# Out-projection of a hybrid backbone step: products take six PSUM banks in turn instead of three

## The chip, the cores and the metric

The kernel runs on one core of a Trainium2 chip. The core has five engines that work from queues of their own: TensorE (PE, matrix products), VectorE (DVE), ScalarE (ACT), GpSimd (POOL) and SyncE (SP, which only issues DMAs here). They share an on-chip memory (SBUF), and PE writes its results to PSUM, eight banks of which each holds 128 x 512 numbers of 32 bits. The metric is the device time of one execution in microseconds (us).

## The reference

One step of a backbone with three parallel token mixers for 128 prompt tokens and 2048 sample tokens, with a width of 1024. The change touches its end alone: the merged branches go through one output projection, the result is scaled by a gate and added to the input, and a last normalisation follows.

```python
    merged = jnp.einsum('btnd,btnd->btd', gt, pb)
    return jnp.einsum('btd,de->bte', merged, w_out), s_f, s_b
...
        h = h + gate[:, None, :] * out
    y_sample = rmsnorm(h, final_g)
```

## The kernel before

All large products are made of 16-bit operands. Each operand is split into a high and a low part, and a product is the sum of three matmuls (high x high, high x low, low x high) for each block of 128 of the inner dimension. The stages follow each other: weights and norms, the input projection with the three mixers (the delta rule's scan runs beside them, paced by hand), the merge, which projects the three branches, weighs them by their gates and writes the merged rows to DRAM (`mrg`), and last the out-projection.

**The out-projection.** The 2048 sample rows are 16 tiles of 128, taken in eight pairs (`PAIRS`: tiles 8 to 15, then 0 to 7). A pair is one loop turn and is computed as a 2 x 2 block product by Strassen's scheme in Winograd's form, in seven products where eight would be needed. `formed(slot, w)` makes one of them: it takes a PSUM bank and issues twelve matmuls of 128 x 128 by 128 x 512 into it. The left operands lie in one half of `xl` (`v`, slots 0 to 6), the right operands in `gq` (weights kept in SBUF) or in `tw` (three weight sums that come back from DRAM into the place of `xh`). The products are asked for in the order of slots 0, 4, 1, 3, 5, 6, 2; slots 3, 5 and 2 use `tw`.

What empties a bank: `joined` (L1738, on DVE) adds a product times `minv` to rows or to a temporary; `held` (L1733, on ACT) copies the first product of a pair out. `added` (POOL) adds temporaries of SBUF to rows. `final` squares the finished rows (ACT, L1696), takes the root (L170, L171), scales them (DVE, L1701) and stores them.

**Work ahead.** While pair i is multiplied, the generator `coming()` is advanced by one step in each product: `pair_operands` forms the 16-bit operands of pair i + 1 in the other half of `xl` (`halved`: L1601 on ACT, L1602 on DVE), and `pair_sums` takes the next pair but one, whose merged rows `m_load` fetches: squares for the scale (L1590, ACT), a reduction (L1591, DVE), and sums of blocks (L1611 to L1614, POOL). The scale itself comes from `scales`: DVE casts the sums of squares to 16 bits (L175, tile `mscb`), PE adds them over the partitions with one matmul of 128 x 1 against ones, and DVE derives the scale (L185 to L189, L1595). That small matmul is the **norm sum** of the pair; `keep=True` holds it at its place in the program.

**What sets the order.** A scheduler orders each engine's queue when the program is built; `tc.high_priority()` around `joined` and `held` and `keep_in_program_order` on some instructions bind it. At run time each engine takes its queue in order, and an instruction waits for semaphores of others.

**The banks.** Six banks hold products: `ps_mm` is one pool of three, and `ps_d` is a list of three pools of one each. Two more (`ps_x`) hold small results such as the norm sums. `bank` takes the next of `ps_d` by the counter `rot`:

```python
        if pl is ps_d:
            rot[0] += 1
            pl = ps_d[rot[0] % 3]
```

Behind the last pair the 128 prompt rows are multiplied with weights scaled block by block (`ublocks`), two times 96 matmuls of 128 x 128 in two banks of `ps_mm`; gate, residual and norm of these rows end the program.

## Time and profile before

| what | us |
|---|---|
| median of three runs | 2180.36 |
| the three runs | 2178.57 to 2188.07 |
| the profiled execution | 2179.54 |
| its span in the profile | 2177.8 |
| PE busy over the span | 2106.6 |
| first product of the out-projection starts | 1997.56 |
| matmuls of 128 x 512 there | 672 |

The span goes from the first to the last instruction of the profiled execution; 1.7 us lie around it. PE counts as busy while any matmul runs, and matmuls overlap, so the busy times of groups of matmuls are not the time that one takes from start to start. Idle time stands in square brackets behind the instruction that ended it, with what released it. All products and norm sums have line L161, the helper that issues matmuls, and are told apart by their tiles.

### The profile page before, as it was taken

How to read it: one execution, taken by the hardware profiler on the slowest of the kernel's cores; microseconds unless marked ns; L12 is line 12 of the kernel's file. 1: busy time of each engine (PE TensorE's matmuls, PEld its weight loads, DVE VectorE, ACT ScalarE, POOL GpSimd, SP SyncE). 2: the span in 40 equal slices, each digit the busy share in tenths (PEclk: the TensorE clock that was granted, in tenths of full speed). 3: DMA queues.
4: the chain of work that ended last, by engine and by line, in shares of the span. 5: the costliest groups of instructions: out<-in, count | busy, mean ns of one | idle time of the engine just before them, and what ended most of it. 6: DMA issues, size and time to landing. Idle time of an engine off the chain costs nothing.

```text
span 2177.8 us, 43136 instructions
## 1 busy us (share of the span) xinstructions
PE 2106.6 (97%) x16275; PEld 1213.6 (56%) x16275; DVE 1412.6 (65%) x3239; ACT 1059.3 (49%) x2462; POOL 730.9 (34%) x873
## 2 busy tenths in 40 slices
PE   7999999999999998999899999999999999999998
PEld 3555444455555587778556556555654444444344
DVE  5746855469978698676665546756664546654775
ACT  3644644345565574554544445755543335323542
POOL 1431533233333324323322223344542222224652
PEclk9999999999999999999999999999999999999999
DMA  8424733266877664444655555867665557534554
GB/s 279 141 92 142 270 112 113 67 200 210 272 219 252 191 193 149 122 127 142 191 183 161 156 165 181 251 186 223 187 193 174 172 157 212 181 126 162 183 172 152
DMA packets 321499, 384.54 MB, mean 177 GB/s; under 512 B 40721, under 2 KB 227322, under 8 KB 318858
## 3 DMA queue, kind: packets, MB, share of 16 engines
q1 hardware_dynamic: 306090, 321.59, 47.9%
q0 software_dynamic: 12752, 51.27, 6.5%
q10 hardware_dynamic: 2448, 8.91, 1.0%
q8 instruction: 128, 2.10, 0.4%
q14 instruction: 81, 0.66, 0.1%
HBM read 246.72 MB, written 134.96 MB: 175 GB/s over the span
## 4 chain that ended last, share of the span: by engine, by line
PE 45%; DVE 7%; DMA 5%; issue 2%; ACT 2%; POOL 1%; SPq 0%; POOLq 0%; DVEq 0%; ACTq 0%
PE b L161 45%; DVE xl L1602 1%; DMA st<-br 1%; DMA mt<-mrg 1%; DVE XB L799 0%; DVE E L800 0%; DMA wst<-in_w_branch_dram 0%; DMA mrg<-mrow 0%; DMA wst<-in_w_in_dram 0%; DMA ES<-ei 0%; DMA skn<-kv 0%; ACT big L1361 0%; DVE S L912 0%; DMA S<-in_state_delta_dram 0%; DMA sq__2210_18514<-qT 0%
## 5 line engine op out<-in xcount | busy, mean ns | idle before, releaser
L161 PE MATMUL b<-xh,whi 128*128 128x512 f16 (+1 forms) x1920 | 651.4, 348 | 1.0 <-ACT sg L1391 0.7
L161 PE MATMUL b<-xl,whi 128*128 128x512 f16 (+1 forms) x1920 | 651.7, 348 | 0.0
L161 PE MATMUL b<-xh,wlo 128*128 128x512 f16 (+1 forms) x1920 | 650.7, 348 | 0.0
L161 PEld LDWEIGHTS <-whi 128*128 128x128 f16 x3840 | 352.2, 98 | 318.4 <-issue 4.8
L161 PEld LDWEIGHTS <-wlo 128*128 128x128 f16 x1920 | 188.4, 98 | 173.8 <-issue 0.8
L161 PE MATMUL b<-big,bhi 128*128 128x512 f16 (+1 forms) x960 | 249.9, 347 | 1.0 <-ACT big L1361 0.8
L161 PEld LDWEIGHTS <-xl 128*128 128x128 f16 x1488 | 139.8, 98 | 107.3 <-issue 18.3
L1402 POOL TENSOR_TENSOR mrow<-mrow,sg 128x512 f32<-128x512 f32 (+1 forms) x80 | 101.5, 1271 | 275.1 <-DVE sg L1401 212.9
L161 PE MATMUL b<-big,blo 128*128 128x512 f16 (+1 forms) x480 | 163.1, 347 | 0.0
L1391 ACT ACTIVATE sg<-b,winv 128x512 f32<-128x512 f32 (+1 forms) x120 | 74.2, 618 | 140.8 <-PE b L161 140.1
L648 POOL TENSOR_TENSOR cy<-cy,raw 128x545 f32<-128x545 f32 (+1 forms) x48 | 73.3, 1555 | 184.2 <-ACT raw L647 184.2
L161 PEld LDWEIGHTS <-xh 128*128 128x128 f16 x1496 | 118.1, 98 | 28.0
L161 PEld LDWEIGHTS <-bhi 128*128 128x128 f16 x960 | 86.6, 98 | 76.4 <-issue 1.5
L211 ACT ACTIVATE wlo<-wst 128x1024 f16<-128x1024 f32 x52 | 55.0, 1058 | 94.7 <-DMA wst<-in_w_in_dram 92.7
L868 POOL COPY T<-ES 32x256 f16<-32x256 f16 x68 | 28.5, 419 | 216.0 <-DMA ES<-ei 208.4
L1401 DVE SCALAR_TENSOR_TENSOR sg<-b,binv,sg 128x512 f32<-128x512 f32 (+1 forms) x80 | 53.3, 666 | 66.1 <-PE b L161 60.6
L161 PE MATMUL b<-whi,xh 128*128 128x128 f16 x544 | 94.8, 221 | 0.0
L161 PE MATMUL b<-wlo,xh 128*128 128x128 f16 x544 | 94.7, 221 | 0.0
L161 PE MATMUL b<-whi,xl 128*128 128x128 f16 x544 | 94.6, 221 | 0.0
L175 DVE CAST wscb<-wss 128x1 bf16<-128x1 f32 x85 | 12.9, 153 | 122.4 <-ACT wlo L211 76.7
L225 DVE SCALAR_TENSOR_TENSOR wlo<-wst,wsc,whi 128x1024 f16<-128x1024 f32 x52 | 70.1, 1353 | 30.7 <-ACT whi L224 29.6
L161 PE MATMUL b<-gq,xl 128*128 128x512 f16 x384 | 85.7, 379 | 1.8 <-DVE hh L1738 1.0
(500 smaller groups left out, 4318.9 us busy)
## 6 DMA issues: line engine op xcount, KB each, us to landing
wst<-in_w_in_dram SPq DMA_DIRECT2D x60, 512.0 KB
qkv<-cy POOLq DMA_DIRECT2D x12, 1089.0 KB, 5.2
st<-br SPq DMA_DIRECT2D x48, 256.0 KB
mrow<-mrg SPq DMA_DIRECT2D x16, 576.0 KB
dc<-dec SPq DMA_DIRECT2D x17, 512.0 KB
kq<-qkv SPq DMA_DIRECT2D x34, 256.0 KB
kv<-tok POOLq DMA_DIRECT2D x17, 512.0 KB, 5.6
n<-n SPq DMA_DIRECT2D x34, 256.0 KB
```

The source lines that it names most:

```text
L161: return PE.matmul(out, l, r, start=start, stop=stop)
L175: V.tensor_copy(sb16, ss)
L211: A.activation(w.lo, st, AF.Square, accum_out=ss)
L225: V.scalar_tensor_tensor(w.lo, st, s, w.hi, ALU.mult, ALU.subtract)
L648: G.tensor_tensor(y[:, c0:c1], y[:, c0:c1], raw[:, 1 + c0:1 + c1], ALU.mult)
L868: G.tensor_copy(T16[rows(a0, b), :, :, b], ES[0:32, :, 2 * a0 + b, :, wT])
L1391: A.activation(sg, ps, AF.Sigmoid, scale=gw.inv)
L1401: V.scalar_tensor_tensor(sg, ps, binv[:, 1:2], sg, ALU.mult, ALU.mult)
L1402: G.tensor_tensor(mr, mr, sg, ALU.add)
L1602: V.scalar_tensor_tensor(lo, src, s, hi, ALU.mult, ALU.subtract)
```

## The change

`formed` no longer tests the counter `rot`, which `bank` moves too. It has a counter of its own, `turn`, that goes 1, 0, 1, 0 and picks `ps_mm` or `ps_d`. Nothing else is edited; lines behind the first hunk move by one.

```diff
     L, R = slice(0, 512), slice(512, D)
+    turn = [0]
     for i_, (ta, tb) in enumerate(PAIRS):
...
         def formed(slot, w):
-            rot[0] += 1
-            ps = bank(ps_mm if rot[0] % 2 else ps_d, [P, 512])
+            turn[0] ^= 1
+            ps = bank(ps_mm if turn[0] else ps_d, [P, 512])
             for k in range(4):
```

The queues of the built programs show what follows from it. First PE, from the fifth product of pair 1 to the second of pair 2, the first row of each product and the norm sum between. A name such as `b_25999` is one product's bank in one use, `xl` the left operand, `gq` or `xh` the right one (`xh` holds `tw`), and `DVE_49` the semaphore that DVE counts up. Before:

```order
L161 MATMUL b_25999<-xh_93,xl_94 128x512 [waits DVE_49]
...
L161 MATMUL b_26022<-gq_23213,xl_94 128x512 [waits DVE_49]
...
L161 MATMUL b_26053<-xh_93,xl_94 128x512 [waits DVE_49]
...
L161 MATMUL b_26083<-gq_23213,xl_94 128x512 [waits DVE_49]
...
L161 MATMUL b_26035<-mscb_26036,ones_2_89 128x1 [waits DVE_49]
...
L161 MATMUL b_26108<-gq_23213,xl_94 128x512 [waits DVE_49]
```

The same place of PE's queue in the changed program:

```order
L161 MATMUL b_25999<-xh_93,xl_94 128x512
...
L161 MATMUL b_26022<-gq_23213,xl_94 128x512
...
L161 MATMUL b_26053<-xh_93,xl_94 128x512 [waits DVE_49]
...
L161 MATMUL b_26083<-gq_23213,xl_94 128x512 [waits DVE_49]
...
L161 MATMUL b_26035<-mscb_26036,ones_2_89 128x1 [waits DVE_49]
...
L161 MATMUL b_26108<-gq_23213,xl_94 128x512
```

The order is the same; three of five products lose their wait for DVE, and the norm sum, in the middle of a product, keeps its own.

Second PE at the end of the loop: the last pair (`b_26901` to `b_26999`) and the first half of the prompt rows' product (`b_27028`, whose weights `whi`, `wlo` are `ublocks`). Before:

```order
L161 MATMUL b_26901<-gq_23213,xl_94 128x512 [waits DVE_49]
...
L161 MATMUL b_27028<-whi_26881,t_3376_26737 128x128 [waits DMAHW5_49]
...
L161 MATMUL b_26918<-gq_23213,xl_94 128x512 [waits DVE_49]
...
L161 MATMUL b_26947<-xh_93,xl_94 128x512 [waits DVE_49]
...
L161 MATMUL b_27028<-wlo_26882,t_3376_26737 128x128
...
L161 MATMUL b_26999<-xh_93,xl_94 128x512 [waits DVE_49]
...
L161 MATMUL b_27028<-whi_26885,t_3376_26737 128x128 [waits DMAHW7_49]
```

In the changed program:

```order
L161 MATMUL b_26901<-gq_23213,xl_94 128x512
...
L161 MATMUL b_26918<-gq_23213,xl_94 128x512
...
L161 MATMUL b_26947<-xh_93,xl_94 128x512 [waits DVE_49]
...
L161 MATMUL b_26999<-xh_93,xl_94 128x512 [waits DVE_49]
...
L161 MATMUL b_27028<-whi_26881,t_3376_26737 128x128 [waits DVE_49]
...
L161 MATMUL b_27028<-whi_26885,t_3376_26737 128x128 [waits DMAHW7_49]
```

Nine of the prompt rows' matmuls stood between the last products; now all 96 of the first half stand behind them.

Third DVE in pair 1, where the operands of pair 2 are formed (L1602) and the products of pair 1 are joined (L1738 before, L1739 now):

```order
-L1602 SCALAR_TENSOR_TENSOR xl_94<-mt_25776,msc_25879,xl_94 128x4x128
-L1738 SCALAR_TENSOR_TENSOR hh_25919<-b_25965,minv_25677,hh_25919 128x512
-L1602 SCALAR_TENSOR_TENSOR xl_94<-mt_25776,msc_25879,xl_94 128x4x128
+L1739 SCALAR_TENSOR_TENSOR hh_25919<-b_25965,minv_25677,hh_25919 128x512
+L1602 SCALAR_TENSOR_TENSOR xl_94<-mt_25776,msc_25879,xl_94 128x4x128 x2
 L1602 SCALAR_TENSOR_TENSOR xl_94<-ost_25906,msc_25879,xl_94 128x4x256
```

One `joined` stands ahead of one L1602 where it stood behind it. It is the only change of order on DVE. On PE there is one more: in pair 0 two matmuls of the sixth product go ahead of the fifth. ACT, POOL and SP have the same order as before.

## The prediction

> **What bounds the kernel now.** I read the page first, then the stage of the change: windows, waits of TensorE (PE), PE's timeline, and what VectorE (DVE) does where PE waits. The page's first table and its chain that ended last:

> ```profile
> PE 2106.6 (97%) x16275; PEld 1213.6 (56%) x16275; DVE 1412.6 (65%) x3239; ACT 1059.3 (49%) x2462; POOL 730.9 (34%) x873
> PE 45%; DVE 7%; DMA 5%; issue 2%; ACT 2%; POOL 1%; SPq 0%; POOLq 0%; DVEq 0%; ACTq 0%
> ```

> PE is busy 97% of the span, so PE bounds the kernel, and only time that PE loses can be won. The out-projection runs from about 1997 us to the end. The windows (columns: length, busy of PE, PEld, DVE, ACT and POOL, granted clock, DMA share, GB/s) show where PE loses some there:

> ```profile
> 1950.00:2000.00 50.00, 50.00 (x262) 23.80 (x261) 15.48 (x26) 14.87 (x30) 19.84 (x20) 1.00 0.36 115
> 2000.00:2050.00 50.00, 43.37 (x199) 19.07 (x198) 35.70 (x52) 21.79 (x40) 28.95 (x24) 1.00 0.68 231
> 2050.00:2100.00 50.00, 46.06 (x199) 20.06 (x198) 40.35 (x59) 22.45 (x46) 31.87 (x24) 0.93 0.51 163
> 2100.00:2150.00 50.00, 49.55 (x238) 22.66 (x237) 38.04 (x65) 21.45 (x39) 21.88 (x19) 1.00 0.60 211
> ```

> PE stands idle 6.6, 3.9 and 0.5 us in these stretches, and in one its clock is below full. PE's waits between 1780 us and the end, whole:

> ```profile
> PE b L161 <- DVE hh L1738: 7.2, 7, 2.8
> PE b L161 <- DVE sg L1738: 1.9, 2, 1.1
> PE b L161 <- DVE xh L1738: 1.9, 1, 1.9
> ```

> Ten waits, 11.0 us, each for a `joined` (L1738), the DVE instruction that empties a bank: the waits for one of three banks. PE's timeline with the longest of them, with the tiny norm sums (`mscb`) that stand in PE's queue, and with the first and last work of the stage (columns: start, length, work, count, idle time before and releaser):

> ```profile
> 1997.56 7.93 PE L161 MATMUL b<-gq,xl 128*128 128x512 f16 x36
> 2007.41 5.34 PE L161 MATMUL b<-xh,xl 128*128 128x512 f16 x24 [1.92 <-DVE xh L1738]
> ...
> 2022.95 0.17 PE L161 MATMUL b<-mscb,ones 128*128 128x1 bf16 x1
> ...
> 2040.52 0.17 PE L161 MATMUL b<-mscb,ones 128*128 128x1 bf16 x1
> ...
> 2049.26 7.03 PE L161 MATMUL b<-xh,xl 128*128 128x512 f16 x24 [2.07 <-DVE hh L1738]
> ...
> 2060.42 0.17 PE L161 MATMUL b<-mscb,ones 128*128 128x1 bf16 x1
> ...
> 2072.91 7.03 PE L161 MATMUL b<-xh,xl 128*128 128x512 f16 x24 [2.80 <-DVE hh L1738]
> ...
> 2082.36 0.17 PE L161 MATMUL b<-mscb,ones 128*128 128x1 bf16 x1
> ...
> 2112.13 5.34 PE L161 MATMUL b<-xh,xl 128*128 128x512 f16 x24 [0.45 <-DVE hh L1738]
> ...
> 2164.16 5.52 PE L161 MATMUL b<-mt,t 128*128 128x128 f16 x96
> ```

> A 128x512 matmul takes (7.93 - 0.38)/35 = 0.2157 us from start to start, a product of twelve 2.59. After the gaps of 2.07 and 2.80 us 24 matmuls take 7.03 us instead of 5.34, because the clock is halved for 3.4 us; after 1.92 us it is not:

> ```profile
> 2049.80:2053.20 3.40, 3.40 (x10) 1.21 (x8) 3.40 (x5) 3.31 (x9) 1.93 (x1) 0.50 0.97 320
> 2073.65:2077.06 3.41, 3.41 (x10) 1.22 (x9) 3.00 (x3) 0.00 (x0) 2.14 (x3) 0.50 0.54 162
> 2007.40:2012.00 4.60, 4.59 (x22) 2.11 (x22) 2.69 (x4) 0.00 (x0) 1.26 (x1) 1.00 0.51 162
> ```

> So PE loses 11.0 us of waits, 10 x 0.16 (a matmul's modelled end lies 0.16 behind the next one's start) and 2 x 1.69 for the clock: 16.0 us. Check: from 1997.56 to 2164.16 are 166.6 us; 56 products, 7 norm sums of 0.03 and the first 96 small matmuls of the tail (0.056 each, from the last row) are 150.5. **16.0 us is the most that more banks can bring.**

> **The change part by part.** It adds and removes no instruction on any engine. The old counter goes up once in `formed` and once more in `bank`, so it is even at every test and each product takes one of the three `ps_d` banks; the new one really alternates. A bank then comes free after six products, not three.

> The order of work moves in three places, each at no cost. Two matmuls go ahead of a neighbour product: same work. One `joined` goes before an L1602 on DVE (0.7 us each); the operand written there belongs to the next pair. At the end, nine small matmuls no longer stand between the last products: the last product then has 192 small matmuls behind it (10.7 us) where it had 183, so the last rows' norm and store keep their cover. No queue of DMAs changes.

> What is late next? With banks free, PE runs to the norm sums: `scales` keeps its matmul in program order, and PE takes its queue in order, so all products behind a norm sum wait for it. It needs DVE's cast of `mscb`:

> ```profile
> 2022.05 0.16 DVE L175 CAST mscb<-mss 128x1 bf16<-128x1 f32 x1
> ...
> 2039.27 0.16 DVE L175 CAST mscb<-mss 128x1 bf16<-128x1 f32 x1
> ...
> 2058.22 0.14 DVE L175 CAST mscb<-mss 128x1 bf16<-128x1 f32 x1
> ...
> 2072.12 0.73 DVE L1738 SCALAR_TENSOR_TENSOR hh<-b,minv,hh 128x512 f32<-128x512 f32 x1
> ...
> 2076.67 0.14 DVE L175 CAST mscb<-mss 128x1 bf16<-128x1 f32 x1
> ```

> DVE runs late by itself here: in the chain of waits nearly all between 2001 and 2073 is DVE, POOL and DMA, hardly any PE. I take the casts at their present times. From DVE's end to PE's start are 0.06 us (2072.12 + 0.73 to 2072.91), so a cast at 2022.05 of 0.16 lets PE go at 2022.27. PE's way through the four marks, without waits for banks:

> Mark 1: 9 products from 1997.56 end at 2020.86; the cast lets PE go at 2022.27, idle 1.41.

> Mark 2: 66 matmuls on, 2036.54; cast 2039.49, idle 2.95. More than 2.07, so the clock drops: 1.69.

> Mark 3: 70 matmuls and 1.69 on, 2056.31; cast 2058.42, idle 2.11.

> Mark 4: 80 matmuls on, 2075.71, or 2077.40 if 2.11 us idle halves the clock too; cast 2076.87.

> The 2.11 us lie between the two gaps that decide (1.92 and 2.07 as listed are 2.08 and 2.23 between the work itself). Two rows are little to set a limit by, so I take the costlier end, the drop. PE then passes mark 4 at 2077.40 where it was 2082.36: 4.96 us won, 5.49 without the drop.

> [...]

> Behind mark 4 two waits are left, both 0.45 (the second is the row at 2112.13), 0.61 with the 0.16 each: 1.22. They go, if DVE follows. The next cast and a `joined` that waits for PE:

> ```profile
> 2085.25 0.75 DVE L1738 SCALAR_TENSOR_TENSOR hh<-b,minv,hh 128x512 f32<-128x512 f32 x1 [0.51 <-PE b L161]
> ...
> 2097.12 0.14 DVE L175 CAST mscb<-mss 128x1 bf16<-128x1 f32 x1
> ```

> At 2085.25 DVE waits for PE, so from there it moves up with PE. If it didn't, the cast would hold PE at 2097.32 where PE passed at 2101.13: 3.8 us stay, plus 0.61 behind it. That is the low end, 4.4.

> Do six banks suffice? Tightest is product 6 of pair 3: it reuses the bank of that pair's first product, emptied at 2072.85, and starts 68 matmuls behind mark 3, at 2073.1 or 2074.8. It fits. And the first weights from `tw`, which PE now wants at 2005.3?

> ```profile
> 1995.56 1.43 SPq L1679 DMA_DIRECT2D xh<-tw  x3
> ...
> 1996.00:2003.00 7.00, 7.00 (x34) 3.17 (x33) 6.54 (x11) 3.98 (x6) 4.04 (x5) 1.00 0.92 338
> ```

> The rows before them (1 MB) and the first megabyte take 2.1 MB / 338 GB/s = 6.2 us: there at about 2002. Were they as late as 2007.41, mark 2 would swallow it.

> **Sum:** 4.96 + 1.22 = 6.2 us (6.7 without the third drop). The profiled execution took 2179.54 us, 0.8 under the median of 2180.36 and inside its three runs. 2179.54 - 6.2 = **2173.3 us**, or 0.3% less.

> **The rivals.** *All waits go* (0.08): 2179.5 - 16.0 = 2163.5. The casts would have to come earlier as PE does. For it: a few DVE gaps end with PE. Against: pair 3's first product starts eight matmuls behind the norm sum at 2060.42, is done by 2065, and DVE takes it at 2072.12, so DVE is late by its own queue.

> *Nothing is won* (0.13): the waits move to the norm sums whole, DVE's casts slip as far as PE runs ahead. 2178 to 2179.5. For it: the four marks show that PE only waits elsewhere. Against: at mark 4 PE passes 5.5 us behind a cast that is already done, and DVE's order hardly changes.

> *Slower* (0.04): DVE itself stretches. Its instructions with two operands in SBUF take either of two times (timeline rows, then minimum, median and maximum in ns of two groups):

> ```profile
> 2022.46 1.26 POOL L1612 TENSOR_TENSOR ost<-ost,mt 128x512 f32<-128x512 f32 x1
> ...
> 2022.52 2.29 DVE L1701 SCALAR_TENSOR_TENSOR xh<-xh,hss,fg 128x1024 f32<-128x1024 f32 x1 [0.32 <-POOL hss L171]
> ...
> L1701 DVE SCALAR_TENSOR_TENSOR hh<-hh,hss,fg x10: 1273/1284/2284, 2044.2 to 2130.5; 128x1024 f32<-128x1024 f32 x10
> L1602 DVE SCALAR_TENSOR_TENSOR xl<-mt,msc,xl x18: 736/745/1761, 2031.1 to 2128.4; 128x512 f16<-128x512 f32 x18
> ```

> Beside a POOL instruction, as here, one costs 1.0 us more (2284 - 1273 ns, 1761 - 736). PE's new timing shifts what meets. Before mark 4 there are three pairs of seven such instructions; by the medians about half are short now. From the seventh stretched one on the gain is gone; all eleven would give 2179.5 - 6.2 + 11 = 2184. [...] Against: DVE's and POOL's orders are almost as before, and what falls together could as well come apart.

> *It does not do what it says* is excluded by the order on PE: the waits at the products' heads go.

> **How the numbers follow.** Forecast 0.75 (2171.3 to 2175.1: gains of 8.2 and 4.4, the first if DVE, which waits less for PE, casts 1.5 us earlier at mark 4), all waits 0.08, nothing 0.13, slower 0.04. The range leaves out the slower case, the extreme of the all-waits case and the last of the nothing case: 2168.5 to 2178.5. A measurement of this kernel can tell about 0.5%, 10.9 us, from no change. Faster by more means under 2169.5: the all-waits case, 0.09 with a corner of the forecast. Slower by more would take over 17 stretched instructions, 0.02. Within: 0.89.

> **What would show it.** PE's waits for L1738 are gone; in their place two or three waits on the norm sums of pairs 1 to 3, for DVE's L175 or `mss`, 1.4, 3 and 2 us, each long one with half a clock window behind it; PE's norm sum of mark 4 at 2077, and no wait of 0.45 later. Wrong would be: waits left at L1738, no wait at norm sums (then more is won), a cast at mark 4 that is not near 2076.7, or a new wait behind mark 4.

## The result, and the profile after

| | before | changed |
|---|---|---|
| median of 8 runs each, us | 2181.58 | 2173.97 |
| range | 2178.57 to 2188.07 | 2170.73 to 2180.15 |
| ratio, with 95% interval | | 0.9967 [0.9956, 0.9978] |
| the profiled execution | 2179.54 | 2173.56 |
| its span | 2177.8 | 2171.8 |
| first product of the out-projection starts | 1997.56 | 1999.00 |
| the second half of the prompt rows' matmuls (the last 96) starts | 2164.16 | 2158.19 |
| the stage between the two | 166.60 | 159.19 |

The change takes 0.33% off. That is less than the 0.5% below which the prediction counted a difference as no change, but the interval excludes 1. The forecast was 2173.3 us.

The page of the changed kernel, its busy times and the chain that ended last:

```profile
PE 2104.7 (97%) x16275; PEld 1208.5 (56%) x16275; DVE 1413.0 (65%) x3239; ACT 1058.2 (49%) x2462; POOL 733.5 (34%) x873
PE 46%; DVE 7%; DMA 5%; ACT 2%; issue 2%; POOL 1%; SPq 0%; DVEq 0%; POOLq 0%; ACTq 0%
```

Nothing to see at this scale: the counts of instructions are the same, and DVE is as busy as before (1412.6), so its instructions didn't stretch. The windows of the changed kernel (columns as before):

```profile
2000.00:2050.00 50.00, 47.28 (x215) 21.02 (x213) 36.39 (x55) 22.54 (x41) 30.16 (x25) 0.97 0.67 237
2050.00:2100.00 50.00, 47.60 (x216) 21.20 (x215) 44.34 (x70) 25.87 (x51) 34.41 (x26) 0.97 0.54 176
2100.00:2150.00 50.00, 50.00 (x235) 22.62 (x233) 37.29 (x60) 18.27 (x35) 20.58 (x18) 1.00 0.56 200
```

PE stood idle 6.6, 3.9 and 0.5 us here and now stands idle 2.7, 2.4 and 0. Its waits from 1780 us to the end are one row where there were three:

```profile
PE b L161 <- DVE mscb L175: 5.1, 2, 2.7
```

All ten waits for a bank are gone, and two waits for DVE's cast have come. PE's timeline with the norm sums of marks 1 to 4 (the loop's first four), the work behind the third, and the first and last work of the stage:

```profile
1999.00 7.93 PE L161 MATMUL b<-gq,xl 128*128 128x512 f16 x36
...
2022.31 0.17 PE L161 MATMUL b<-mscb,ones 128*128 128x1 bf16 x1
...
2039.47 0.16 PE L161 MATMUL b<-mscb,ones 128*128 128x1 bf16 x1 [2.72 <-DVE mscb L175]
...
2058.64 0.16 PE L161 MATMUL b<-mscb,ones 128*128 128x1 bf16 x1 [2.40 <-DVE mscb L175]
...
2058.67 2.71 PE L161 MATMUL b<-xh,xl 128*128 128x512 f16 x8
2061.17 8.84 PE L161 MATMUL b<-gq,xl 128*128 128x512 f16 x36
...
2077.62 0.17 PE L161 MATMUL b<-mscb,ones 128*128 128x1 bf16 x1
...
2158.19 5.52 PE L161 MATMUL b<-mt,t 128*128 128x128 f16 x96
```

Marks 2 and 3 wait, 1 and 4 don't, and behind mark 3 the clock is halved for a while: 8 matmuls take 2.71 us instead of 1.89, and 36 take 8.84 instead of 7.93. DVE's casts for the four marks:

```profile
2021.96 0.16 DVE L175 CAST mscb<-mss 128x1 bf16<-128x1 f32 x1
...
2039.26 0.16 DVE L175 CAST mscb<-mss 128x1 bf16<-128x1 f32 x1
...
2058.45 0.14 DVE L175 CAST mscb<-mss 128x1 bf16<-128x1 f32 x1
...
2076.82 0.14 DVE L175 CAST mscb<-mss 128x1 bf16<-128x1 f32 x1
```

They stand within 0.25 us of before (2022.05, 2039.27, 2058.22, 2076.67), although PE began the stage 1.44 us later and waits for no bank. Counted from the stage's start they come 1.2 to 1.5 us earlier than before. PE no longer waits for DVE to empty a bank; it runs ahead to the next thing that it needs from a late DVE.

### The profile page after: what moved, and what is told of

It is laid out like the page before. It is cut to its first block, busy times and chain, and to the rows that moved or that the text cites. A ratio compares the mean times of both kernels' runs of the same rounds, so it can differ in the third digit from the quotient of the medians.

```text
span 2171.8 us, 43136 instructions
## 1 busy us (share of the span) xinstructions
PE 2104.7 (97%) x16275; PEld 1208.5 (56%) x16275; DVE 1413.0 (65%) x3239; ACT 1058.2 (49%) x2462; POOL 733.5 (34%) x873
## 4 chain that ended last, share of the span: by engine, by line
PE 46%; DVE 7%; DMA 5%; ACT 2%; issue 2%; POOL 1%; SPq 0%; DVEq 0%; POOLq 0%; ACTq 0%
PE b L161 45%; DMA st<-br 1%; DVE xl L1602 1%; DMA wst<-in_w_branch_dram 1%; DMA N<-n 1%; DVE XB L799 0%; DMA wst<-in_w_in_dram 0%; DMA mt<-mrg 0%; DVE E L800 0%; DVE big L1362 0%; DMA mrg<-mrow 0%; DMA ES<-ei 0%; DMA S<-in_state_delta_dram 0%; DVE o L928 0%; ACT big L1361 0%
## 5 line engine op out<-in xcount | busy, mean ns | idle before, releaser
L161 PE MATMUL b<-xh,whi 128*128 128x512 f16 (+1 forms) x1920 | 651.8, 348 | 1.3 <-DVE mrow L1398 0.6
L161 PE MATMUL b<-xh,wlo 128*128 128x512 f16 (+1 forms) x1920 | 651.3, 348 | 1.2 <-DVE wlo L225 1.2
L161 PE MATMUL b<-xl,whi 128*128 128x512 f16 (+1 forms) x1920 | 652.0, 348 | 0.0
L161 PEld LDWEIGHTS <-whi 128*128 128x128 f16 x3840 | 351.0, 98 | 320.3 <-issue 7.1
L161 PEld LDWEIGHTS <-wlo 128*128 128x128 f16 x1920 | 187.8, 98 | 176.4 <-issue 2.4
L161 PE MATMUL b<-big,bhi 128*128 128x512 f16 (+1 forms) x960 | 250.1, 348 | 1.5 <-ACT big L1361 1.1
L161 PEld LDWEIGHTS <-xl 128*128 128x128 f16 x1488 | 139.3, 98 | 100.7 <-issue 9.5
L161 PE MATMUL b<-big,blo 128*128 128x512 f16 (+1 forms) x480 | 163.3, 347 | 0.0
L161 PEld LDWEIGHTS <-xh 128*128 128x128 f16 x1496 | 116.9, 97 | 28.1
L161 PEld LDWEIGHTS <-bhi 128*128 128x128 f16 x960 | 86.5, 98 | 76.9 <-issue 1.6
L175 DVE CAST wscb<-wss 128x1 bf16<-128x1 f32 x85 | 12.9, 153 | 125.0 <-ACT wlo L211 78.9
L161 PE MATMUL b<-whi,xh 128*128 128x128 f16 x544 | 93.2, 219 | 0.0
L161 PE MATMUL b<-wlo,xh 128*128 128x128 f16 x544 | 93.2, 219 | 0.0
L161 PE MATMUL b<-whi,xl 128*128 128x128 f16 x544 | 93.2, 219 | 0.0
L161 PE MATMUL b<-gq,xl 128*128 128x512 f16 x384 | 88.3, 387 | 0.0
```

Of the source, the lines that this page charges most:

```text
L161: return PE.matmul(out, l, r, start=start, stop=stop)
L175: V.tensor_copy(sb16, ss)
```

## The experiments

The stage, from the first product to the first of the last 96 small matmuls (the second half of the prompt rows' product), is the yardstick. Its start moved between 1993 and 2007 us in the profiles of these kernels, whose work ahead of it is the same, so totals scatter by more than most edits bring. Each row is one profiled execution; 150.5 us is the work of PE in the stage, and what is above it is lost. "Half" counts the stretches of 3.41 us at half clock in the stage.

| run | stage, us | PE's waits, us (times) | half | ratio to before, 95% |
|---|---|---|---|---|
| before | 166.6 | 11.0 (10) | 2 | |
| changed | 159.2 | 5.1 (2) | 2 | 0.9967 [0.9956, 0.9978] |
| changed_again | 158.6 | 5.8 (3) | 1 | 0.9965 [0.9953, 0.9977] |
| three_of_one_pool | 164.3 | 10.5 (10) | 1 | 1.0000 [0.9991, 1.0009] |
| four_banks | 158.7 | 5.7 (3) | 1 | 0.9975 [0.9962, 0.9988] |
| first4_pairs | 161.2 | 8.2 (4) | 1 | 0.9986 [0.9974, 0.9998] |
| last4_pairs | 160.6 | 7.2 (7) | 1 | 0.9974 [0.9964, 0.9984] |
| late_norm_three | 164.7 | 12.6 (9) | 0 | 0.9973 [0.9963, 0.9983] |
| late_norm_six | 163.7 | 10.7 (5) | 1 | 0.9988 [0.9976, 1.0000] |
| squares_first | 158.0 | 4.7 (1) | 2 | 0.9959 [0.9945, 0.9973] |
| early_rows_three | 159.9 | 6.7 (6) | 1 | 0.9980 [0.9968, 0.9992] |
| early_rows_six | 154.9 | 2.5 (1) | 1 | 0.9956 [0.9941, 0.9972] |
| early_rows_squares | 152.6 | 1.8 (1) | 0 | 0.9946 [0.9926, 0.9967] |
| early_rows_squares_again | 152.6 | 1.9 (1) | 0 | 0.9942 [0.9928, 0.9956] |

In each row waits, 0.16 us for each of them and the half-clock time (up to 1.7 us for a stretch) add up to the stage less 150.5 within 0.3 us. So nothing else is lost.

### How much is the change, and does the pool matter?

The changed kernel again, unedited:

> The changed kernel once more, unedited, beside the kernel before on the same chip, as the yardstick of the next runs and of how far a stage's length differs from run to run. If its gain is that of the stage (7.4 us less from the first product to the prompt rows' matmuls): ratio 0.9965, stage near 159.2 us, waits only at the norm sums of marks 2 and 3. If part of the first result was chance: stage over 161 us or ratio above 0.998.

It repeats: 158.6 us and 0.9965. A third, shorter wait came at mark 4 (1.1 us), and only one of its long waits halved the clock: behind 2.66 us at mark 2 30 matmuls took 8.32 us where 6.63 are their time at full clock, behind 2.11 us at mark 3 none was slower.

All products from one pool of three banks:

```diff
-            turn[0] ^= 1
-            ps = bank(ps_mm if turn[0] else ps_d, [P, 512])
+            ps = bank(ps_mm, [P, 512])
```

> All products take the three banks of ps_mm; ps_d is unused. Control. Theory (what counts is after how many products a bank is used again): as the kernel before, stage 165.5 to 167.5 us, waits on L1738's successor of 10 to 12 us in about ten, ratio 0.9985 to 1.001. Rival (the pool or the counter itself mattered): stage under 163 us.

The total doesn't move, and the ten bank waits are there as before. The stage is 1.2 us under what I expected: with three banks it varies too, because here one gap halved the clock (2.38 us; one of 2.03 did not) where two did in the profile of before (2.07 and 2.80 us). Which pool holds the three banks is of no account.

Four banks' distance:

```diff
-    turn = [0]
+    turn = [-1]
...
-            turn[0] ^= 1
-            ps = bank(ps_mm if turn[0] else ps_d, [P, 512])
+            turn[0] += 1
+            ps = bank(ps_d if turn[0] % 4 else ps_mm, [P, 512])
```

> Three of four products take ps_d, each fourth ps_mm: a bank is used again after four products at the earliest. Theory: one product more is 2.59 us more room, the ten bank waits were 2.80 or less, so at most one of a few tenths of a us is left and the loss sits at the norm sums as with six: stage 159 to 161 us, ratio 0.996 to 0.998. Rival (five or six are needed): bank waits of over 2 us in sum stay, stage 162 to 166 us.

PE's waits in the stage of this run:

```profile
PE b L161 <- DVE mscb L175: 4.4, 2, 2.3
PE b L161 <- DVE hh L1739: 1.3, 1, 1.3
```

One bank wait is left of ten, of 1.3 us where a few tenths were expected; the loss sits at the norm sums as with six. A distance of four products between two uses of a bank does nearly all of it.

### Where in the loop is the gain made?

Six banks in the first four pairs only, and in the last four only:

```diff
-            turn[0] ^= 1
-            ps = bank(ps_mm if turn[0] else ps_d, [P, 512])
+            turn[0] ^= i_ < 4
+            ps = bank(ps_mm if turn[0] and i_ < 4 else ps_d, [P, 512])
```

```diff
-            turn[0] ^= 1
-            ps = bank(ps_mm if turn[0] else ps_d, [P, 512])
+            turn[0] ^= i_ >= 4
+            ps = bank(ps_mm if turn[0] and i_ >= 4 else ps_d, [P, 512])
```

> Six banks in pairs 0 to 3 only; pairs 4 to 7 keep three. Theory (the gain is made before mark 4, the norm sum of pair 4): PE has no bank wait up to mark 4, waits there for the casts of marks 2 and 3 (2.7 and 2.4 us, each with a half-clock window), passes mark 4 at about 2077.6 as in the changed kernel, and the two waits of 0.45 behind it come back. Gain over the kernel before 4.7 of about 6, ratio about 0.998. Rival (the gain comes from the end of the loop, where the nine small matmuls moved, or from the last pairs): mark 4 no earlier than 2081, ratio 0.9995 to 1.000.

> Six banks in pairs 4 to 7 only; pairs 0 to 3 keep three. Theory: the eight long bank waits ahead of mark 4 stay (about 10 us of idle time and two half-clock windows), only the two waits of 0.45 behind it go: gain 1.2 us, ratio about 0.9994, mark 4 at 2082. Rival (gain of the end of the loop): ratio 0.997 as in the changed kernel, with mark 4 still at 2082.

The first pairs do nearly what was expected, but with one half-clock stretch where two were. PE's waits in that run:

```profile
PE b L161 <- DVE mscb L175: 6.6, 2, 3.8
PE b L161 <- DVE hh L1739: 1.6, 2, 1.1
```

The bank waits come back only behind mark 4, which PE passes 78.7 us into the stage, as in the changed kernel (2077.62 - 1999.00 = 78.6) and not as before (2082.36 - 1997.56 = 84.8). The wait at mark 2, 2.81 us, halved no clock here, so PE came to mark 3 earlier and waited 3.82 us there instead of 2.40, for a cast at the same distance from the stage's start (59.6 us, 59.5 in the changed kernel): the cast sets when PE passes. From mark 4 to the end of the stage 82.5 us pass, against 80.6 in the changed kernel and 81.8 before.

The last pairs were a miss: 1.2 us expected, 6.0 found. The reason is in PE's timeline of that run, in pair 3:

```profile
2065.87 1.89 PE L161 MATMUL b<-xh,xl 128*128 128x512 f16 x8
2067.59 11.39 PE L161 MATMUL b<-gq,xl 128*128 128x512 f16 x52
2078.82 5.34 PE L161 MATMUL b<-xh,xl 128*128 128x512 f16 x24
```

Three products with `gq` are 36 matmuls; here stand 52. With its banks free, the scheduler took 16 matmuls of pair 4 ahead of that product of pair 3 which waited 2.80 us before. They fill the wait: 2.80, 0.16 and the 1.69 us of a half-clock stretch go beside the two waits of 0.45, 4.65 + 1.22 = 5.9. This run says nothing against the gain's place; it shows that an edit of the banks is an edit of PE's order too, which has to be read before such a run is sized.

### Is the norm sum's place in PE's queue the fault?

In the changed kernel PE waits at norm sums, though the products behind them need nothing of that scale. So the norm sum is put behind the second product of the next pair (core of the edit):

```diff
+        def finish():
+            with tc.issue_after(lastmm[0].ins):
+                s, inv = scales(None, orp, "lsc", s16)
...
+            pending.append(finish)
...
         def coming():
+            if pending:
+                for _ in range(1):
+                    yield
+                pending.pop()()
```

> Six banks, and the norm sum of each loop pair stands in PE's queue behind the second product of the next pair, with the same cast ahead of it on DVE. Same work in all. Theory (in the changed kernel PE waits at the norm sums because they stand at the head of its queue, though the products behind them need nothing of DVE): the waits on mscb (2.7 and 2.4 us) and both half-clock windows (1.69 us each) go, 5.1 + 0.3 + 3.4 = 8.8 us is the most; PE runs into banks or operands again in part, so 3 to 8.8 us less than the changed kernel, ratio to the kernel before 0.993 to 0.996. Rival (DVE sets the pace whatever PE does, and the gain is used up): the waits move whole to operands (xl of the next pair, now formed later since the scale comes later) or to banks; ratio 0.997 to 1.000.

> The kernel before, with three banks, and the norm sums behind the second product of the next pair, as in the run with six. Theory (with three banks the banks bind first, the norm sums wait for nothing): the ten waits for L1738 stay at about 11 us, ratio 0.999 to 1.001; were the scale's later time to matter, slower by 1 to 4 us. Rival (the norm sum's place costs time whatever the banks): faster by 3 us or more, ratio under 0.9985.

With six banks it lost: 163.7 us where 150 to 156 would have followed. DVE in that run, from one cast to the next (the cast's tile is called `lscb` here):

```profile
2063.33 0.16 DVE L175 CAST lscb<-mss 128x1 bf16<-128x1 f32 x1
...
2065.41 0.15 DVE L170 TENSOR_SCALAR hss<-hss 128x1 f32<-128x1 f32 x1 [1.26 <-ACT ojk L1724]
...
2068.42 2.28 DVE L1729 SCALAR_TENSOR_TENSOR hh<-hh,hss,fg 128x1024 f32<-128x1024 f32 x1 [2.18 <-POOL hss L171]
...
2073.95 0.15 DVE L185 COPY lsc<-b 128x1 f32<-128x1 f32 x1
...
2083.45 0.16 DVE L175 CAST lscb<-mss 128x1 bf16<-128x1 f32 x1
```

And PE's longest wait in that run:

```profile
2131.22 0.16 PE L161 MATMUL b<-mscb,ones 128*128 128x1 bf16 x1 [5.19 <-DVE mscb L175]
```

The norm sum is made at 2063.54, but DVE takes it at 2073.95: its order has changed, and it now stops in every pair for the last normalisation of the rows just finished, 1.26 and 2.18 us in these rows. One pair takes it 20.1 us from cast to cast, and PE's work for a pair is 84 x 0.2157 + 0.03 = 18.15. So from the third of the loop's norm sums on DVE falls behind in every pair, and PE waits for its cast at four of the six norm sums of pairs (0.56 to 1.85 us). The longest wait, 5.19 us of the 10.7, is another: the norm sum of the prompt rows stands in the middle of the last pair but one and holds PE until DVE has made its cast. The edit changed DVE's order with PE's, so the run doesn't tell what the place of the norm sum costs by itself; it shows that moving it, done this way, leaves PE waiting for DVE. With three banks the run behaves as theory said (nine bank waits, 12.6 us); its total ratio, 0.9973, is lower than the 1.9 us of its stage explain (0.9991), and that difference stays open.

### Why are the casts late?

If they are late by their place in DVE's queue, issuing the squares, their sum and the cast ahead of the next operands must help (core of the edit; a second hunk moves the cast in `pair_sums` ahead of its `yield`):

```diff
-                yield from pair_operands(i_ + 1, *summed[i_ + 1])
+                ops_ = pair_operands(i_ + 1, *summed[i_ + 1])
+                if i_ and nx is not None:
+                    sums_ = pair_sums(*nx)
+                    next(sums_)
+                    yield
+                    yield from ops_
+                    yield from sums_
+                    return
+                yield from ops_
```

> Six banks; from pair 1 on the squares, their reduction and the cast for the next pair but one are issued ahead of the operands of the next pair, not behind. Same work. On DVE the reduction and cast of mark 2 then stand by the scale of mark 1, some 9 us earlier; the norm sum of mark 2 stands 18 matmuls earlier on PE. Theory (the casts were late by their place in DVE's queue, not for their inputs): no wait at mark 2 (2.72 and 0.16 us and the half clock of 1.69 go, 4.6 us); at mark 3 PE comes at about 2050.8 on the changed kernel's scale, the cast at 2050 to 2053, so a wait of 0 to 2.3 us, with or without a half-clock window; later marks none. Stage 151 to 155 us, ratio to the kernel before 0.993 to 0.995. Rival (DVE's work as a whole, or the squares' input, sets the pace): the wait moves to mark 3 or to ACT and the operands whole, stage 158 to 161 us, ratio 0.996 to 0.998.

PE's only wait in that run is at mark 3, and the DVE rows there:

```profile
2049.78 0.16 PE L161 MATMUL b<-mscb,ones 128*128 128x1 bf16 x1 [4.69 <-DVE mscb L175]
```

```profile
2022.74 0.74 DVE L1751 SCALAR_TENSOR_TENSOR sg<-b,minv,sg 128x512 f32<-128x512 f32 x1
...
2035.10 0.15 DVE L170 TENSOR_SCALAR hss<-hss 128x1 f32<-128x1 f32 x1 [0.51 <-ACT ojk L1697]
...
2038.71 2.29 DVE L1702 SCALAR_TENSOR_TENSOR hh<-hh,hss,fg 128x1024 f32<-128x1024 f32 x1 [0.44 <-POOL hss L171]
...
2046.73 2.28 DVE L1702 SCALAR_TENSOR_TENSOR hh<-hh,hss,fg 128x1024 f32<-128x1024 f32 x1 [0.22 <-POOL hss L171]
...
2049.59 0.14 DVE L175 CAST mscb<-mss 128x1 bf16<-128x1 f32 x1
```

The wait at mark 2 is gone and mark 3 waits 4.69 us instead of 2.40. These are DVE's only waits between 2022.74 and the cast, 1.2 us in 27: it works through a backlog, and the new order alone brings little (158.0 us). That is the rival, and it points back in time, to where the backlog began. In the changed kernel the trace shows it in three steps: the wait of SP's queue, ACT's and DVE's:

```profile
SPq L1710 <- DMA mrg<-mrow: 12.5, 1, 12.5
```

```profile
2017.86 0.63 ACT L1590 ACTIVATE t<-mt 128x512 f16<-128x512 f32 x1 [12.98 <-DMA mt<-mrg]
```

```profile
2020.40 0.15 DVE L170 TENSOR_SCALAR hss<-hss 128x1 f32<-128x1 f32 x1 [4.91 <-ACT ojk L1696]
```

SP holds the load of `fg` until a store of the merge has landed, and behind it in SP's queue stand the merged rows of pair 2. ACT stands idle 13.0 us before it can square them, the square of pair 0's finished rows stands behind the first of these squares on ACT, and DVE, in order, waits 4.9 us for that square. So load pair 2's rows ahead of `fg`, into buffers that pair 0's rows have left:

```diff
+    early = []
+    with tc.issue_after(lead[0]):
+        early.append([m_load(t, wp, ["wst"]) for t in PAIRS[2]])
...
-            nx = [m_load(t, op, ["mt"]) for t in PAIRS[i_ + 2]] if i_ + 2 < len(PAIRS) else None
+            nx = (early.pop() if early else [m_load(t, op, ["mt"]) for t in PAIRS[i_ + 2]]) if i_ + 2 < len(PAIRS) else None
```

> Six banks; the merged rows of pair 2 are loaded into the two buffers that held pair 0's rows (free by 1996), right behind the weights tw in SP's queue, and no longer behind the load of fg, which waits 12.5 us for the last merge's store. Same work. Theory (the root of the late casts is one idle time of DVE: in the changed kernel it waits 4.9 us at 2020.40 for the square of pair 0's rows, which stands on ACT behind squares that wait 13.0 us for pair 2's rows; from there DVE is busy without a gap up to mark 3): that idle time goes, the casts of marks 2 and 3 come 3 to 5 us earlier, the waits there (2.7 and 2.4 us) and their half-clock windows go. Stage 150.5 to 154 us, ratio to the kernel before 0.992 to 0.995. Rival (DVE's work alone is too much for these pairs, the idle time at the start does not matter): stage 157 to 160 us with a wait at mark 3, ratio 0.996 to 0.998.

> The same early load of pair 2's rows in the kernel before, with three banks. Theory (the bank waits behind the first pair were DVE's lateness too, so the early load helps three banks as well): the waits for L1738 between 2024 and 2074 fall from 9 us to 1 to 5 us, stage 154 to 161 us, ratio 0.994 to 0.9975. Rival (three banks are too few by themselves): waits of 9 us or more stay, stage 164 to 167 us, ratio 0.999 to 1.001.

> Both: six banks, pair 2's rows early, and the squares ahead of the operands from pair 1 on. Theory: as the early load alone or up to 1 us better, since one of the two is enough to have the cast ahead of PE at mark 2 and the load alone gives DVE the time it lacks at mark 3: stage 150.5 to 153 us. Rival (DVE's throughput): wait at mark 3 as in the run with the squares ahead, stage 157 to 158 us.

> The run with both edits once more, for its total time. If the shorter stage (152.6 us, against 158.6 to 159.2 of the changed kernel) is real, ratio to the kernel before 0.993 to 0.9955, stage 152 to 154.5 us (the upper end if the wait at mark 2 or 3 now halves the clock). If it was chance: ratio 0.9965 and stage near 157 us.

With six banks the stage falls to 154.9 us, 0.9 above the expected range and well under the rival's. ACT, DVE and PE of that run, whose stage begins at 2007.29:

```profile
2021.50 0.63 ACT L1590 ACTIVATE t<-wst 128x512 f16<-128x512 f32 x1 [8.17 <-DMA wst<-mrg]
```

```profile
2024.76 0.16 DVE L1591 TENSOR_REDUCE mss<-mss 128x1 f32<-128x4 f32 x1 [3.14 <-ACT t L1590]
...
2044.28 0.14 DVE L175 CAST mscb<-mss 128x1 bf16<-128x1 f32 x1
...
2060.01 0.14 DVE L175 CAST mscb<-mss 128x1 bf16<-128x1 f32 x1
```

```profile
2044.47 0.16 PE L161 MATMUL b<-mscb,ones 128*128 128x1 bf16 x1 [2.46 <-DVE mscb L175]
```

The rows come 14.2 us into the stage (2021.50 - 2007.29), where they came 18.9 (2017.86 - 1999.00), 4.7 us earlier and not as early as hoped, so DVE still waits 3.1 us for them. But the casts of marks 2 and 3 come 37.0 and 52.7 us into the stage, and came 40.3 and 59.5: 3.3 and 6.7 earlier. Mark 3 no longer waits; mark 2 does, since the new order has its norm sum 14 matmuls earlier. With three banks the same load brings the stage to 159.9 us, nearly as far as six banks do alone, with 3.7 us of bank waits left between 2024 and 2074 where 9 were (its total, 0.9980, misses the expected 0.9975). So the bank waits and the norm-sum waits share a cause, the idle time of DVE at the start of the stage, and either cure takes less than half of the 16.0 us. It is not the only cause. The two cures bring 6.7 and 7.4 us singly and 11.7 together; in the changed kernel DVE also waits 1.22 and 2.29 us between the casts of marks 2 and 3 (at 2041.29 for ACT's square, at 2044.40 for POOL's root of finished rows). And the early load changed the order with the arrival: mark 1's cast comes 17.7 us into the stage instead of 23.0. Order alone was not enough in the run above, but what the arrival does by itself isn't shown.

Both edits and six banks give 152.6 us, twice; PE's waits in the second run:

```profile
PE b L161 <- DVE mscb L175: 1.9, 1, 1.9
```

Its median is 2167.07 us where the kernel before had 2180.20 on the same chip, and the changed kernel (changed_again) 2173.76 on that chip. **This version beats both kernels**: 0.9942 [0.9928, 0.9956] and 0.9946 [0.9926, 0.9967], against 0.9967 and 0.9965 for the change alone. The intervals of these ratios touch or overlap; the stages, 152.6 against 158.6 to 159.2, lie clearly apart.

## Why the prediction was right, step by step

- **16.0 us is the most that more banks can bring.** Right as an account, and as a bound: with the other edits 14.0 us of them went.
- **The change really alternates, and six banks suffice.** Right: no wait on L1739. A distance of four products is nearly enough.
- **PE runs to the norm sums.** Right: the only waits left are for L175's `mscb`.
- **The casts stay at their present times.** In the profiled execution they did, within 0.25 us, and that was in part luck. The stage's start moves from run to run, and the casts move with it: in changed_again the stage starts at 2005.38, and the casts of marks 2 and 3 come at 2045.57 and 2064.68. Counted from the start, the casts of marks 1 to 4 came 1.2 to 1.5 us earlier than before (mark 2: 40.26 instead of 41.71), and in changed_again 1.3 to 1.6 earlier. With three banks in another run (three_of_one_pool) mark 2's came at 41.10. Pair 2's rows reached ACT 18.9 us into the stage instead of 20.4; why is not shown. The reason given, that DVE is late by its own queue, held for mark 2, but mark 1's cast waits for those rows, and the prediction did not look for what made DVE late.
- **Mark 1, idle 1.41.** Not there: PE was at mark 1 at 2022.31, with the cast done at 2022.12. The stage began 1.44 us later while the cast stayed at 2021.96 (2022.05 before). In changed_again PE doesn't wait at mark 1 either.
- **Marks 2 and 3, idle 2.95 and 2.11, each with a half-clock stretch.** Measured 2.72 and 2.40, each with one. That the third drop came was right in this execution, by luck: the rule behind it, a limit between gaps of 1.92 and 2.07 us, does not hold in these runs: in early_rows_three a wait of 2.40 us halved nothing (see the last section). In the second profile of the same kernel a wait of 2.11 us at mark 3 halved nothing.
- **Mark 4 at 2077.40, 4.96 us won.** 2077.62 and 4.74.
- **Two waits of 0.45 behind mark 4, 1.22 us.** From mark 4 to the end of the stage 80.57 us pass, and 81.80 before: 1.23.
- **Sum 6.2 us, 2173.3.** The profiled execution lost 2179.54 - 2173.56 = 6.0. The stage itself lost 7.4 (8.0 in changed_again), and by medians the kernel lost 7.6. So the mechanism was right and the sum 1 to 2 us low: up to mark 4 the stage won 84.80 - 78.62 = 6.18 us where 4.96 were forecast, since the casts, counted from the stage's start, came earlier than the prediction took them. That the profiled execution met 2173.3 within 0.3 us is luck, for its stage began 1.44 us later and hid this. The upper end of the forecast, 8.2 us for casts 1.5 us earlier at mark 4, had allowed for it.
- **The rivals.** That all waits go did not come true, for the reason given: it takes earlier casts, and early_rows_squares, which has them, comes near it. That nothing is won and that DVE stretches are both out: 5.1 us of waits replaced 11.0, and DVE's busy time is the same to 0.4 us. Nor is it always DVE that takes longer where DVE and POOL work at once: in the profile of before L1701 took 2.28 us at 2094.26 beside 1.26 of L1742 on POOL, and at 2130.46 it took 1.27 beside 2.30 of L1742.

## What to carry to other kernels

When a wait goes, look for the next thing that the engine needs from the same late partner: read its queue for the next instruction with a wait; here the gain was the difference of the two, with the clock's share. Then follow the late partner back to the first idle time of its own: here one load behind a queue's blocked head, two engines away, was worth 6.7 us with three banks and 4.3 with six, where the banks alone were worth 7.4. And before an experiment is sized, compare the order of the queues: freeing banks in four pairs moved products of one pair into another and turned an expected gain of 1.2 us into one of 6.

## What the hardware showed

How long one gap is doesn't tell in this stage whether the clock halves: in early_rows_three 24 matmuls took 7.03 us behind a wait of 2.07 and 5.34 behind one of 2.40. How much of a window PE works, by its modelled busy time, does tell in the windows that follow. They are of before, changed, changed_again, first4_pairs, squares_first and early_rows_squares_again (second column the length, third PE's busy time; the clock is the third number from the end). Those of changed_again, first4_pairs and squares_first are counted in steps of 3.4133 us from a window of the same run at half clock (at 2045.85, 2061.27 and 2048.17). The last run has none in its stage: where the grid lies there isn't shown, and its row is a stretch of the same length in which its wait of 1.89 us begins.

```profile
2005.38:2008.79 3.41, 1.49 (x8) 0.66 (x7) 3.30 (x5) 0.00 (x0) 1.11 (x2) 1.00 0.91 378
2008.79:2012.20 3.41, 3.41 (x18) 1.52 (x17) 1.41 (x2) 0.00 (x0) 0.58 (x1) 1.00 0.44 105
2046.34:2049.76 3.42, 1.35 (x7) 0.55 (x6) 3.26 (x10) 2.81 (x4) 0.55 (x1) 1.00 0.49 198
2049.76:2053.17 3.41, 3.41 (x10) 1.23 (x9) 3.41 (x5) 3.32 (x9) 1.90 (x1) 0.50 0.97 320
```

```profile
2035.70:2039.11 3.41, 1.05 (x5) 0.39 (x4) 3.41 (x4) 1.07 (x4) 2.25 (x1) 1.00 0.14 43
2039.11:2042.52 3.41, 3.05 (x9) 1.12 (x9) 1.76 (x6) 1.39 (x3) 2.49 (x2) 0.50 0.58 159
```

```profile
2062.92:2066.33 3.41, 1.46 (x8) 0.70 (x8) 3.38 (x9) 0.12 (x1) 0.92 (x1) 1.00 0.54 154
2066.33:2069.74 3.41, 3.41 (x18) 1.57 (x16) 1.09 (x6) 3.41 (x6) 3.06 (x3) 1.00 0.01 2
```

```profile
2037.38:2040.79 3.41, 1.60 (x8) 0.62 (x7) 3.41 (x4) 1.67 (x6) 2.89 (x2) 1.00 0.42 124
2040.79:2044.20 3.41, 2.41 (x13) 1.11 (x13) 2.16 (x7) 1.15 (x2) 2.49 (x2) 1.00 0.55 159
```

```profile
2048.17:2051.58 3.41, 1.80 (x6) 0.70 (x6) 3.41 (x6) 0.00 (x0) 2.19 (x2) 0.50 0.45 173
2051.58:2055.00 3.42, 3.42 (x10) 1.22 (x9) 1.64 (x8) 2.56 (x5) 3.31 (x4) 0.50 0.44 156
```

```profile
2031.72:2035.13 3.41, 1.82 (x9) 0.72 (x8) 3.41 (x5) 0.00 (x0) 3.41 (x3) 1.00 0.41 168
```

At full clock, 1.05 or 1.35 us of work in a window were followed by half clock in the next, and 1.46, 1.49, 1.60 and 2.41 were not. Half clock also followed on 0.33 us (squares_first, at 2044.76), 0.37 (first4_pairs, 2057.86), 0.74 (before, 2070.24), 0.75 (changed_again, 2042.44) and 1.01 (changed, 2056.18). All other windows of the stage in the profiles of before and changed held over 2.4 us, and none of them was followed by half clock. The wait of 2.81 us in first4_pairs, which falls across two windows, halved nothing (1.60 and 2.41 us of work), and the shorter one of 2.46 in early_rows_six did: the 8 and 36 matmuls behind it took 2.54 and 9.01 us instead of 1.89 and 7.93. The one window here with more work that was followed by another half (1.80 us, squares_first) was itself at half clock and held 6 matmuls, where 1.82 us at full clock held 9. A limit between 1.35 and 1.46 us of work in 3.41 fits all these windows at full clock; it is an estimate from them, and no experiment was made to set it by itself. Elsewhere in the same profiles modelled busy time doesn't decide as cleanly: 1.90 us in the window at 22.24 of before were followed by half clock, 1.74 in the one at 707.91 of changed were not. So the same kernel can gain or lose up to 1.7 us a time (24 matmuls in 7.03 us or in 5.34) by where its waits fall on the grid, which may be part of why its runs differ.
